# Two groups of zero matmuls, 55 of 128 columns, re-cut as 14 of 512 columns

## The chip, the cores and the metric

One core of a Trainium2 chip. The metric is device time in microseconds (us), the median of several executions; lower is better. "Span" is the stretch that the profile covers, about 2 us less than the time. An execution is "slow" when it lies over 1.5% above the fastest of its kernel; all comparisons below use fast executions. In the lines of the profile, PE is TensorE, PEld its weight loads, DVE VectorE, ACT ScalarE, POOL GpSimd and SP SyncE; L84 is line 84 of the kernel.

## The reference

A 3x3 convolution with padding 1, 16 images of 64 channels and 64x64 points, 128 output channels. The weights are 90% zeros, but the kernel treats them as dense.

```python
batch, c_in, h, w, c_out, k = 16, 64, 64, 64, 128, 3
for b, co, ci, kh, kw:   # five loops in the original
    if weight[co, ci, kh, kw] != 0:
        output[b, co] += weight[co, ci, kh, kw] * x_pad[b, ci, kh:kh+h, kw:kw+w]
```

x is 16.8 MB in f32, the output 33.6 MB in f32.

## The kernel before

Images are worked on in pairs, one on each half of TensorE's 128 rows. x is cast to bf16 while it is loaded, except the first 32 rows of the first pair, which are loaded as f32 and cast by VectorE and ScalarE, to be ready earlier. Before the first convolution the weights are loaded, cast, transposed on TensorE and combined. The parts concerned (cuts marked with ...):

```python
xs = [x_pool.tile([128, H, W], BF16, name=f"x{p}") for p in range(NP)]
...
nc.sync.dma_start(out=w_sb, in_=weight.rearrange("o i kh kw -> o (i kh kw)"))
x_head = o_pool.tile([128, H, W], FP32, name="o")
nc.sync.dma_start(out=x_head[:, 0:HEAD, :], in_=pair(0)[:, 0:HEAD, :])
nc.gpsimd.dma_start(out=xs[0][:, HEAD:H, :], in_=pair(0)[:, HEAD:H, :])
...
for p in range(1, EARLY):           # EARLY = 4
    load(p)
load(EARLY, 0, CUT)

idle_rhs = const_pool.tile([128, 128], BF16, name="idle_rhs")
nc.vector.memset(idle_rhs, 0.0)
idle_ps = psum_pool.tile([128, 128], FP32, name="ps")

def keep_busy(n):
    for _ in range(n):
        nc.tensor.matmul(idle_ps, idle_rhs, idle_rhs, start=True, stop=True)

keep_busy(27)                       # first group, while w is on its way
...                                 # casts and nine transposes of w
keep_busy(28)                       # second group, while x is on its way
cast_x(nc.scalar.copy, 9, 18)
...
for p in range(NP):                 # 8 pairs: convolution, then
    ...                             #   2 MB of output per image
            elif p > 1 and blk == 3 and p + EARLY - 1 < NP:
                load(p + EARLY - 1) # later loads are paced by the work
    if not last:
        for n in range(2):
            nc.sync.dma_start(out=out[2 * p + n], in_=o[n])
```

The zero matmuls write a tile in PSUM, the memory that takes the results of TensorE, and nobody reads it. They keep TensorE busy so that its clock is up when the convolution starts.

## Time and profile before

| | before |
|---|---|
| time, median (3 runs at first, then 6) | 126.27, 126.31 us |
| span of the profiled execution | 124.3 us |
| TensorE busy; VectorE busy | 88%; 66% |
| HBM traffic | 50.62 MB |
| convolution starts; last matmul ends | 7.38; 110.7 us |
| first output issued; last output issued | 21.86; 112 us |

The filler has these two rows among the groups (line, engine, operation, shape and count; busy us, mean ns of one; idle time before and what ended it):

```profile
L84 PE MATMUL ps<-idle_rhs 128*128 128x128 bf16 x55 | 4.8, 265 | 1.0 <-DVE idle_rhs L79 1.0
L84 PEld LDWEIGHTS <-idle_rhs 128*128 128x128 bf16 x55 | 4.4, 122 | 1.0 <-DVE idle_rhs L79 1.0
```

4.8 us of TensorE, every matmul with a weight load of its own. And one row of the DMA queues, to be compared later (queue, kind: transfers, MB, share of 16 engines): 8 blocks of 16 KB of instructions are fetched while the kernel runs.

```profile
q8 instruction: 8, 0.13, 0.4%
```

### The profile page before, as it was taken

What the parts mean: (1) busy time and instruction counts of PE and PEld (TensorE: products, weight loads), DVE (VectorE), ACT (ScalarE), POOL (GpSimd) and SP (SyncE); (2) the same over time, 40 slices, a digit from 0 to 9 for tenths busy, and PEclk for the clock granted to TensorE, in tenths of its full rate; (3) what the DMA queues carried; (4) which work ended last, traced back from release to release, by engine and by line L of the source; (5) the groups of instructions that cost most, each with busy time, mean ns of one, the idle gap of its engine ahead of it and who ended that gap; (6) DMA issues with size and microseconds to landing.
All of it is one profiled execution on the core that took longest, in us unless ns stands there. A gap on an engine that the chain in (4) does not pass through costs nothing.

```text
span 124.3 us, 2549 instructions
## 1 busy us (share of the span) xinstructions
PE 108.9 (88%) x1030; PEld 59.8 (48%) x1030; DVE 82.2 (66%) x135; ACT 39.0 (31%) x71; POOL 41.1 (33%) x46
## 2 busy tenths in 40 slices
PE   6989999999999999999999999999999999960000
PEld 6845555555555555555555555555555555520000
DVE  0354677877787778777877787778888788870000
ACT  4545323333333333333333333333333333310000
POOL 6428253533353335333533333343333310000000
PEclk9999999999999999999999999999999999998555
DMA  4999999999999999999999999999999999999991
GB/s 130 348 225 216 214 219 213 203 418 311 346 409 411 316 298 327 432 319 329 308 422 332 308 306 409 432 432 430 427 438 416 438 427 432 422 419 414 424 409 82
DMA packets 4196, 42.93 MB, mean 345 GB/s; under 512 B 472, under 2 KB 472, under 8 KB 984
## 3 DMA queue, kind: packets, MB, share of 16 engines
q1 hardware_dynamic: 2888, 34.90, 66.8%
q0 software_dynamic: 1296, 7.86, 30.8%
q8 instruction: 8, 0.13, 0.4%
q14 instruction: 4, 0.03, 0.1%
HBM read 17.07 MB, written 33.55 MB: 407 GB/s over the span
## 4 chain that ended last, share of the span: by engine, by line
PE 82%; DMA 5%; DVE 1%; issue 1%; DVEq 0%; SPq 0%
PE ps L148 82%; DMA o<-in_x_dram 5%; DVE o L181 1%; DVEq L240 0%; DVE x L99 0%; SPq L60 0%; DVEq L181 0%
## 5 line engine op out<-in xcount | busy, mean ns | idle before, releaser
L181 DVE TENSOR_TENSOR o<-ps,pc 128x512 f32<-128x512 f32 x124 | 77.7, 685 | 22.2 <-PE ps L148 19.8
L148 PE MATMUL ps<-x,wT 64*128 64x504 bf16 (+3 forms) x780 | 88.8, 373 | 0.6 <-DVE x L99 0.6
L148 PEld LDWEIGHTS <-wT 64*128 64x128 bf16 x966 | 54.8, 94 | 48.9 <-issue 0.6
L167 POOL TENSOR_TENSOR s<-x 128x512 bf16<-128x512 bf16 x31 | 35.5, 1149 | 57.6 <-PE ps L148 40.2
L174 ACT COPY pc<-ps 128x512 f32<-128x512 f32 x62 | 33.3, 590 | 64.0 <-issue 61.8
L148 PE MATMUL ps<-s,wT 64*128 64x512 bf16 (+1 forms) x186 | 25.7, 377 | 0.0
L84 PE MATMUL ps<-idle_rhs 128*128 128x128 bf16 x55 | 4.8, 265 | 1.0 <-DVE idle_rhs L79 1.0
L84 PEld LDWEIGHTS <-idle_rhs 128*128 128x128 bf16 x55 | 4.4, 122 | 1.0 <-DVE idle_rhs L79 1.0
L68 POOL DMA_DIRECT2D x<-in_x_dram x8 | 4.4, 559 | 0.0
L103 DVE CAST w_bf<-w_sb 128x192 bf16<-128x192 f32 (+1 forms) x4 | 1.1, 345 | 2.7 <-DMA w_sb<-in_weight_dram 2.7
L162 DVE COPY o<-ps 128x512 f32<-128x512 f32 x2 | 1.4, 692 | 2.0 <-PE ps L148 2.0
L161 ACT COPY o<-ps 128x512 f32<-128x512 f32 x2 | 1.2, 586 | 2.4 <-PE ps L148 2.4
L99 ACT CAST x<-o 128x576 bf16<-128x576 f32 (+1 forms) x2 | 1.5, 802 | 1.1 <-DMA o<-in_x_dram 1.1
L99 DVE CAST x<-o 128x576 bf16<-128x576 f32 x1 | 0.5, 459 | 2.1 <-DMA o<-in_x_dram 2.1
L103 ACT ACT_TABLE_LOAD x1 | 1.3, 1283 | 0.7 <-PEq L229 0.7
L103 ACT CAST w_bf<-w_sb 128x64 bf16<-128x64 f32 (+1 forms) x2 | 0.7, 416 | 1.6 <-DMA w_sb<-in_weight_dram 1.6
L109 PE MATMUL ps<-ident,w_bf 128*128 128x128 bf16 x9 | 1.0, 276 | 0.1
L113 DVE TENSOR_TENSOR wT<-ps,wT 128x384 bf16<-128x384 f32 x2 | 1.0, 546 | 0.0
L109 PEld LDWEIGHTS <-w_bf 128*128 128x128 bf16 x9 | 0.7, 120 | 0.5 <-DVE w_bf L103 0.5
L63 POOL DMA_DIRECT2D x<-in_x_dram x1 | 0.7, 693 | 0.8 <-POOLq L229 0.8
L79 DVE MEMSET idle_rhs<- 128x64 uint32 x1 | 0.1, 112 | 0.8 <-PEq L229 0.8
L122 ACT CAST wT<-ps 128x384 bf16<-128x384 f32 x1 | 0.5, 478 | 0.4 <-PE ps L109 0.4
(8 smaller groups left out, 1.9 us busy)
## 6 DMA issues: line engine op xcount, KB each, us to landing
out_dram<-o SPq DMA_DIRECT2D x14, 2048.0 KB, 17.9
x<-in_x_dram POOLq DMA_DIRECT2D x6, 1024.0 KB, 15.7
out_dram<-o SPq DMA_DIRECT2D x4, 1024.0 KB, 12.0
o<-in_x_dram SPq DMA_DIRECT2D x1, 1024.0 KB
x<-in_x_dram POOLq DMA_DIRECT2D x1, 640.0 KB, 14.3
x<-in_x_dram POOLq DMA_DIRECT2D x1, 512.0 KB, 7.6
x<-in_x_dram POOLq DMA_DIRECT2D x1, 384.0 KB, 25.2
w_sb<-in_weight_dram SPq DMA_DIRECT2D x1, 288.0 KB
```

The costliest lines, as they stand in the source:

```text
L68: nc.gpsimd.dma_start(out=xs[p][:, a:b, :], in_=pair(p)[:, a:b, :])
L84: nc.tensor.matmul(idle_ps, idle_rhs, idle_rhs, start=True, stop=True)
L99: copy(out=xs[0][:, a:b, :], in_=x_head[:, a:b, :])
L103: copy(out=w_bf4[:, g, a:b, :], in_=w_v[:, k : k + b - a, :])
L109: nc.tensor.matmul(wps[:, j, :], src, ident, start=True, stop=True)
L113: nc.vector.tensor_tensor(out=wT[:, g], in0=wps, in1=wT[:, G1], op=SUB)
L148: nc.tensor.matmul(ps[n][:, lo:hi, c_lo:c_hi], tap(g, kw, n), src[q, a:b:step, c_lo + kw - 1 : c_hi + kw - 1], start=(i == 0), stop=(i == ...
L161: nc.scalar.copy(out=o[0][:, r0 : r0 + rows, :], in_=ps[0])
L162: nc.vector.tensor_copy(out=o[1][:, r0 : r0 + rows, :], in_=ps[1])
L167: nc.gpsimd.tensor_tensor(out=s, in0=xs[p][:, r0 : r0 + 16 : 2, :], in1=xs[p][:, r0 + 1 : r0 + 16 : 2, :], op=ADD)
L174: nc.scalar.copy(out=c, in_=shared[n])
L181: nc.vector.tensor_tensor(out=o[n][:, first : r0 + 16 : 2, :], in0=ps[n], in1=pc[n], op=ADD)
```

## The change

The same busy time with fewer instructions: 7 + 7 matmuls of 512 columns (7168 columns) for 27 + 28 of 128 (7040). The weights of a zero matmul stay 128 columns.

```diff
-    idle_rhs = const_pool.tile([128, 128], BF16, name="idle_rhs")
+    idle_rhs = const_pool.tile([128, 512], BF16, name="idle_rhs")
     nc.vector.memset(idle_rhs, 0.0)
-    idle_ps = psum_pool.tile([128, 128], FP32, name="ps")
+    idle_ps = psum_pool.tile([128, 512], FP32, name="ps")
 
     def keep_busy(n):
         for _ in range(n):
-            nc.tensor.matmul(idle_ps, idle_rhs, idle_rhs, start=True, stop=True)
-
-    keep_busy(27)
+            nc.tensor.matmul(idle_ps, idle_rhs[:, 0:128], idle_rhs, start=True, stop=True)
+
+    keep_busy(7)
@@ after the transposes
-    keep_busy(28)
+    keep_busy(7)
```

## The prediction

> **What bounds the kernel now.** I read the page first for the transfers, because TensorE's 88% busy alone would suggest that TensorE sets the time. The rows of the 40 slices (3.1 us each), and what went to and from HBM:
>
> ```profile
> PE   6989999999999999999999999999999999960000
> DMA  4999999999999999999999999999999999999991
> GB/s 130 348 225 216 214 219 213 203 418 311 346 409 411 316 298 327 432 319 329 308 422 332 308 306 409 432 432 430 427 438 416 438 427 432 422 419 414 424 409 82
> HBM read 17.07 MB, written 33.55 MB: 407 GB/s over the span
> PE 82%; DMA 5%; DVE 1%; issue 1%; DVEq 0%; SPq 0%
> ```
>
> See three things. PE stops four slices before the end, while DMA is at 9 from the second slice to the last but one. The rate is about 215 GB/s where only loads run (slices 3 to 8) and about 425 where only outputs run. And the chain (last line, of its summary by engine) names PE for 82%, but it ends at the last compute instruction and says nothing of the 12 us after that. The 215 is not a slow DMA: x is loaded as f32 and lands as bf16, and the rate counts the bytes that land. HBM traffic is 50.62 MB (17.07 + 33.55) against 42.93 MB in the queues' total; the missing 7.69 MB is about the 7.86 MB of the converting queue, counted once instead of twice. So in HBM bytes the early rate is about 430 as well. 50.62 MB at 427 GB/s (the rate of a late slice) takes 118.5 us; the DMA begins to move at about 1.5 us and is done at about 122.5. That leaves some 2 us of 121 without full traffic. The transfers bound this kernel, not TensorE.
>
> Second, busy shares in four stretches (columns: stretch, length, the five compute engines in us with counts, granted clock, DMA share, GB/s):
>
> ```profile
> 1.50:24.50 23.00, 22.28 (x223) 13.78 (x223) 13.41 (x25) 9.19 (x17) 11.48 (x15) 1.00 1.02 232
> 24.50:61.00 36.50, 36.50 (x346) 19.40 (x344) 28.55 (x46) 12.67 (x24) 14.41 (x14) 1.00 1.02 354
> 61.00:105.00 44.00, 44.00 (x416) 23.37 (x414) 34.60 (x56) 14.22 (x28) 14.72 (x14) 1.00 1.01 400
> 105.00:120.00 15.00, 5.66 (x54) 2.78 (x50) 5.56 (x9) 2.12 (x4) 0.00 (x0) 0.80 1.00 422
> ```
>
> The next to last column is full in all four; in the last stretch PE works 5.66 of 15 us and the outputs drain.
>
> Third, the timeline of the start, where the change lies (start, duration, engine, line, operation; in brackets the idle time before it and what ended it):
>
> ```profile
> 0.82 0.11 DVE L79 MEMSET idle_rhs<- 128x64 uint32 x1 [0.82 <-PEq L229]
> 0.99 3.06 PE L84 MATMUL ps<-idle_rhs 128*128 128x128 bf16 x27 [0.99 <-DVE idle_rhs L79]
> 3.62 1.14 DVE L103 CAST w_bf<-w_sb 128x192 bf16<-128x192 f32 x4 [2.68 <-DMA w_sb<-in_weight_dram]
> 4.17 1.04 PE L109 MATMUL ps<-ident,w_bf 128*128 128x128 bf16 x9
> 5.05 1.73 PE L84 MATMUL ps<-idle_rhs 128*128 128x128 bf16 x28
> 6.87 0.46 DVE L99 CAST x<-o 128x576 bf16<-128x576 f32 x1 [2.11 <-DMA o<-in_x_dram]
> 7.38 3.99 PE L148 MATMUL ps<-x,wT 64*128 64x512 bf16 x36 [0.61 <-DVE x L99]
> ```
>
> The zero matmuls are not needed for any result; they fill the time in which weights and image arrive. The first 27 take 3.06 us, 113 ns each, and individually 314 ns from start to modelled end; the 28 later ones take 1.73 us, 62 ns each, individually 219 ns. The durations change among the nine transposes, so TensorE gets its full speed at about 4.9 us, though the granted clock reads 1.00 from the first slice: that column does not show this warm-up. PE then waits 0.61 us for the cast of x, which waited for its load to land at 6.85. This fixes 7.38 whatever the filler does, so long as the filler ends before it.
>
> **What the Trainium skill says.** "TensorE: Matmul & The Clock Gate", section "What's actually happening", says that the array runs at half clock until it has been busy for one window of about 3.4 us, and that the window runs freely. The trace agrees in size: busy from 0.99, fast at about 4.9, 3.9 us. Its section "Wait — 56ns, not 53.3ns?" gives the distance from start to start: N/1.2 ns cold and N/2.4 + 2.5 ns warm, so 107 and 56 ns for 128 columns, 427 and 216 ns for 512. The trace has 106 ns (3.06 less the last one's 0.31, over 26 distances) and 56 ns (1.73 less 0.22, over 27). For 512 columns I use the page's figures as estimates; nothing with 512 columns on the full array stands in this trace. "VectorE: DVE Perf Modes", section "Zero memsets can be issued as uint32 (trn2)", says one cycle per element: the trace shows the uint32 form, 64 elements in 112 ns. "DMA: Bandwidth & Descriptors", section "Where 436 GB/s comes from", puts the ceiling of the ports at 435 GB/s; slices at 427 to 438 are at it.
>
> **The change part by part.** It removes 55 zero matmuls (27 + 28), each with its weight load, and puts 14 (7 + 7) in their place. The columns streamed go from 7040 to 7168, nearly the same array time by design. PE gets 82 instructions fewer; ACT, POOL and SP keep the order they had; DVE gets only a larger memset.
>
> Memset: 256 elements in place of 64. 192 more elements at one cycle of the VectorE's 0.96 GHz (the specification in the skill's "Trainium Kernel Development and Optimization", NeuronCore Architecture) are 0.20 us, so 0.31 us. The first filler starts at about 1.19 in place of 0.99. DVE has nothing else until 3.62: no cost there.
>
> First filler: cold, 7 x 427 = 2.99 us from first start to the earliest next start, so the array is free at 4.18; before, 27 x 106 = 2.86, free at 3.85. The transposes, held until 4.17 by the cast of the weights, may start about 0.02 us later. On the path of PE, nothing worth a sum.
>
> Second filler: 7 x 216 = 1.51 us against 28 x 56 = 1.57. It starts at about 5.07, the array is free at 6.58 and the last one ends near 6.75 (before 6.78). Still ahead of 7.34, when the cast of x releases the convolution. PE's wait there goes from 0.61 to about 0.6 us.
>
> Sum on the path: 0 at the first real matmul, and hence 0 in every output's issue time. Total: 126.27 + 0.0.
>
> **The rivals.** *The clock warms one window later.* The filler starts 0.2 us later, and the window runs freely; if the start falls just outside a window, full speed comes at about 8.3 in place of 4.9 (one 3.41 us window more). Then the second filler is cold: 7 x 427 = 2.99 us from 5.07, to 8.06, and the convolution starts 0.7 us late. That would move the chain of PE by 0.7 us and a little more for a few slow matmuls, up to 1 us. For it: 3.9 us in the trace is 0.5 more than one window, so the window began at about 1.5 and 1.19 still lies before it, but other executions have other phases. Against any effect on time: the first output is issued at 21.86, and the DMA is still working on the loads issued at the start until about 24.5, when the rate goes from 160 to 393 GB/s. So 2.6 us of lateness is hidden there. At the other end, about 7.0 MB move after 105.0, of which 4.19 MB are the last pair's; the other 2.8 MB are a backlog of 6.7 us at that time. Worth: 0 to +0.3 us.
>
> *Fewer instructions help.* 82 fewer on PE, and their fetching, could free the start of a queue. But the loads of w and x are issued by SP and POOL at 0.74 to 4.6 us without waiting for PE, and instruction queues take 0.5% of the DMA. Worth: 0 to -0.2 us.
>
> *Fewer, longer matmuls count as less activity, or the clock falls between the last filler and the convolution.* The idle gap there stays 0.6 us, which before did no harm: the 36 matmuls after it take 3.99 us, 111 ns each, the pace of the whole kernel. If it did fall, some 3.4 us at half speed cost about 1.7 us of PE, again below the 2.6 us of slack. Worth: 0 to +0.5 us.
>
> **Range and chances.** All three rivals end at a full DMA queue, so the spread is that of executions: before has 126.22 to 126.40. Another build on another turn of the chip may lie some tenths away. I predict 126.25 us, 8 in 10 between 125.9 and 126.7. Over 2% either way is 2.5 us, for which I see no mechanism: faster by over 2% 0.005, within 0.99, slower 0.005.
>
> **What would show it right or wrong.** In the changed profile: the memset near 0.31 us; the first filler about 1.2 to 4.35 by its modelled end (seven of about 600 ns cold); transposes at 4.17 to 4.25; the second filler done before 6.9; the first real matmul at 7.38 within 0.1, released by the cast of x; DMA digits unchanged, end of traffic near 122.5. Wrong would be a first real matmul after 7.5 or the first 36 spread over clearly more than 4 us (late clock), and, if the time then moved by as much, my claim that the DMA queue hides it. A change of the time with an unchanged start would mean that I have mistaken what bounds the transfers.

## The result, and the profile after

126.35 us median of 6 runs (126.10 to 126.55) against 126.31 (126.22 to 126.42). The ratio is 1.000, 95% interval 0.9987 to 1.0013. Ratios here are the mean time of one kernel's fast runs over that of the other's of the same rounds, so not quite the ratio of the medians quoted.

The start after (timeline: start, duration, engine, line, operation):

```profile
0.86 0.27 DVE L79 MEMSET idle_rhs<- 128x256 uint32 x1 [0.86 <-PEq L229]
1.19 3.17 PE L84 MATMUL ps<-idle_rhs 128*128 128x512 bf16 x7 [1.19 <-DVE idle_rhs L79]
4.26 1.16 PE L109 MATMUL ps<-ident,w_bf 128*128 128x128 bf16 x9
5.26 1.67 PE L84 MATMUL ps<-idle_rhs 128*128 128x512 bf16 x7
7.38 3.99 PE L148 MATMUL ps<-x,wT 64*128 64x512 bf16 x36 [0.44 <-DVE x L99]
```

The filler starts 0.20 us later, the second group ends at 6.93, and the convolution starts at 7.38 as before, released by the same cast of x. Its first 36 matmuls take 3.99 us, as before: the clock is up. The stretches that the prediction shows, and the transfers (the page's row of DMA, then its row of the instruction queue):

```profile
1.50:24.50 23.00, 22.56 (x185) 11.41 (x185) 13.43 (x25) 9.20 (x17) 11.54 (x15) 1.00 1.02 232
105.00:120.00 15.00, 5.66 (x54) 2.78 (x50) 5.56 (x9) 2.11 (x4) 0.00 (x0) 0.82 0.99 421
DMA  4999999999999999999999999999999999999991
q8 instruction: 7, 0.11, 0.3%
```

The weight loads in the first stretch fall from 13.78 to 11.41 us; DMA share and rate stay. One thing differs that I had not counted: the instruction queue fetched 7 blocks of 16 KB instead of 8. It returns in the experiments.

### The profile page after: what moved, and what is told of

Same layout as the page of the kernel before. It is cut to its first block, busy times and chain, and to the rows that moved or that the text cites. A ratio compares the mean times of both kernels' runs of the same rounds, so it can differ in the third digit from the quotient of the medians.

```text
span 124.5 us, 2467 instructions
## 1 busy us (share of the span) xinstructions
PE 109.0 (88%) x989; PEld 57.1 (46%) x989; DVE 82.4 (66%) x135; ACT 39.0 (31%) x71; POOL 41.2 (33%) x46
## 4 chain that ended last, share of the span: by engine, by line
PE 82%; DMA 5%; DVE 1%; issue 1%; DVEq 0%; SPq 0%
PE ps L148 82%; DMA o<-in_x_dram 5%; DVE o L181 1%; DVEq L240 0%; DVE x L99 0%; SPq L60 0%; DVEq L181 0%
## 5 line engine op out<-in xcount | busy, mean ns | idle before, releaser
L181 DVE TENSOR_TENSOR o<-ps,pc 128x512 f32<-128x512 f32 x124 | 77.8, 685 | 22.1 <-PE ps L148 19.8
L84 PE MATMUL ps<-idle_rhs 128*128 128x512 bf16 x14 | 4.8, 505 | 1.2 <-DVE idle_rhs L79 1.2
L84 PEld LDWEIGHTS <-idle_rhs 128*128 128x128 bf16 x14 | 1.6, 121 | 3.2 <-issue 1.4
```

Source lines behind the costliest of these rows:

```text
L84: nc.tensor.matmul(idle_ps, idle_rhs[:, 0:128], idle_rhs, start=True, stop=True)
L181: nc.vector.tensor_tensor(out=o[n][:, first : r0 + 16 : 2, :], in0=ps[n], in1=pc[n], op=ADD)
```

## The experiments

The theory: the transfers run without a break from the start to the end, so the end moves only where the DMA stands idle; and the convolution's start is set by x, not by the filler. Main rival: TensorE sets the end. All kernels below are edits of the changed kernel unless stated. The kernel before ran beside each on the same chip; its median was 126.26, 126.36 and 126.34 us in the three batches.

### No filler at all

```diff
-    keep_busy(7)
+    keep_busy(0)
@@ second group
-    keep_busy(7)
+    keep_busy(0)
```

> Both zero-matmul groups removed (0 in place of 7 and 7); memset and tiles stay. Theory (the transfers bound the kernel, the start of the convolution has about 2.6 us of slack): TensorE is idle before 4.2 and from about 5.3 to 7.4, so the convolution starts at 7.38 but at half speed until one busy window of some 3.4 us has passed, up to two with the free phase; PE is 1.7 to 3.4 us late from then on, first output issued at 23.6 to 25.3 in place of 21.86; time +0.0 to +0.8 us. Rival (PE sets the end): time +1.7 to +3.4 us. Rival (the filler does nothing for the clock): first 36 matmuls still 4 us, no lateness, time +0.0.

Five fast runs of 126.42 to 128.22 us, one slow; ratio 1.0061 (1.0011 to 1.0111), some 0.8 us. In the profiled run (127.79 us):

```profile
4.27 1.22 PE L109 MATMUL ps<-ident,w_bf 128*128 128x128 bf16 x9 [4.27 <-DVE w_bf L103]
7.35 6.80 PE L148 MATMUL ps<-x,wT 64*128 64x512 bf16 x36 [1.85 <-DVE x L99]
```

The first 36 matmuls take 6.80 us in place of 3.99, so the filler is worth 2.8 us of TensorE in this execution; the first output is issued at 24.65, 2.8 us late. The span is 126.0, only 1.5 us more than the 124.5 of the changed kernel: part is hidden. The rival that the filler does nothing falls. The mean loss is inside my 0.0 to 0.8, but single runs are beyond it; the slack must be smaller than 2.6 us.

### Delays of the convolution

More zero matmuls in the second group delay the convolution. Its own matmuls then run at full speed (the first 36 in 3.98 us in all four). One thing besides changes: all four fetch 8 blocks of instructions, as the kernel before does, where the changed one fetches 7.

```diff
-    keep_busy(7)
+    keep_busy(17)    # delay_2;  29 in delay_4, 57 in delay_10, 14 in delay_1
```

> Second group 17 in place of 7: 10 x 216 ns more, array free at about 8.93, so the convolution starts 1.55 us later, at full speed. Theory: inside the slack of 2.6 us at the first output, time +0.0 (under 0.3 us). Rival (PE sets the end): +1.55 us, 1.2%.

> Second group 29 in place of 7: convolution starts at about 11.5, 4.1 us later, at full speed. Theory: 2.6 us of that are hidden, so +1.5 us (0.9 to 2.1). Rival (PE sets the end): +4.1. Rival (only the backlog of 6.7 us at the end is the slack): +0.0.

> Second group 57 in place of 7: convolution starts at about 17.6, 10.2 us later. Theory: the loads issued at the start are through at about 24.5, the first output is issued at about 32, so the DMA stands idle for 7.5 us and the end moves by as much: +7.5 us (7 to 8.3). Rival (PE sets the end): +10.2 us. Rival (only the backlog at the end counts as slack, 6.7 us at 105): +3.5 us.

> Second group 14 in place of 7: array free at about 8.3, convolution 0.9 us later. The runs with larger delays gave spans of first output issue + 101.3 to 101.6 us, against 124.3 to 124.5 without delay, so the slack at the first output is about 1.2 us, not 2.6. Theory with that slack: time +0.0 to +0.3. Rival (PE sets the end, the smaller gains being noise): +0.9 us.

| kernel | convolution starts | first output issued | span | span less first issue | median us | ratio to before |
|---|---|---|---|---|---|---|
| before | 7.38 | 21.86 | 124.3 | 102.4 | 126.31 | 1 |
| changed | 7.38 | 21.86 | 124.5 | 102.6 | 126.35 | 1.000 |
| delay_1 | 8.93 | 23.42 | 125.4 | 102.0 | 126.41 | 1.0019 |
| delay_2 | 8.79 | 23.28 | 124.9 | 101.6 | 126.83 | 1.0053 |
| no filler | 7.35 | 24.65 | 126.0 | 101.4 | 127.2 (fast) | 1.0061 |
| delay_4 | 11.90 | 26.39 | 127.7 | 101.3 | 129.56 | 1.0253 |
| delay_10 | 17.71 | 32.20 | 133.6 | 101.4 | 135.22 | 1.0719 |

The times in columns two to five are of the profiled execution, the last two of all runs. (That of delay_1 was one of two with an execution over 127 us: its second group started with slow matmuls, so the delay was 1.55 us there, not 0.9; the other four were 126.21 to 126.50. Delay_4 began its second group with slow matmuls too, and its delay was 4.5 us where 4.1 was expected; that of delay_10 was 10.3.) From a delay of 2.8 us on, the end follows the first output one to one, 101.4 us behind it. Without delay the end is at 124.4. The two meet at a first output at 124.4 - 101.4 = 23.0 us: the slack is about 1.2 us, not 2.6. Delay_4 was outside my 0.9 to 2.1 (it cost 3.2 us), delay_10 outside my 7 to 8.3 (it cost 9.1); "TensorE sets the end" would have been 4.1 and 10.2, "only the backlog at the end counts" 0 and 3.5. Delay_2 was to cost under 0.3 us and cost 0.6. Each of these numbers misses. On delay_4 and delay_10 mine miss by 1.7 and 1.6 us, and those of "TensorE sets the end" by only 0.9 and 1.1, so these two numbers alone do not decide for me. What speaks against that rival is that about the same 1.2 us is missing from both (4.5 and 10.3 us of measured delay, 3.2 and 9.1 of cost) and that it had 1.55 for delay_2; the next experiment tests it directly. A slack of 1.2 us fits delay_4 and delay_10 within 0.2 and delay_2 within 0.4. The traced execution of delay_1 ends 0.6 us later than this slack gives; why is open.

Where the missing 1.4 us of slack lie shows the idle DMA of delay_10 (stretches: as above, the last two columns are DMA share and GB/s):

```profile
22.00:23.00 1.00, 1.00 (x12) 0.45 (x10) 0.45 (x1) 0.94 (x3) 0.49 (x1) 1.00 0.81 162
24.00:25.00 1.00, 1.00 (x14) 0.41 (x12) 1.00 (x3) 0.00 (x0) 0.00 (x0) 1.00 0.64 123
25.00:26.00 1.00, 1.00 (x12) 0.48 (x10) 1.00 (x3) 0.38 (x1) 0.24 (x1) 1.00 0.03 6
32.20:33.00 0.80, 0.80 (x11) 0.39 (x8) 0.51 (x1) 0.80 (x2) 0.80 (x1) 1.00 0.00 0
33.00:34.00 1.00, 1.00 (x14) 0.49 (x10) 0.69 (x2) 0.14 (x1) 0.83 (x2) 1.00 1.25 524
```

Between the issue of the first output at 32.20 and the first traffic at 33.0 lie 0.8 us, which I had left out; and the engines run dry unevenly before 24.5 (share 0.81 between 22 and 23, 0.64 between 24 and 25). The first is measured; that the second makes the remaining 0.6 us is the rest of the sum, not measured by itself.

### Less to load

Pairs 4 to 7 use the images of pairs 0 to 3 again. The result is wrong (relative error 1.0); all compute instructions and outputs stay, 8.4 MB of HBM reads go.

```diff
-    xs = [x_pool.tile([128, H, W], BF16, name=f"x{p}") for p in range(NP)]
+    xs = [x_pool.tile([128, H, W], BF16, name=f"x{p}") for p in range(4)]
+    xs = xs + xs
@@
-    load(EARLY, 0, CUT)
@@ and the two later calls of load in the loop over pairs
```

> Wrong result on purpose: pairs 4 to 7 use the images of pairs 0 to 3 again, so 8.4 MB less is read from HBM; every compute instruction and every output stays. Theory: PE keeps its times (convolution 7.38 to about 110), but the DMA has no backlog left; the last two outputs are issued at 111.4 to 112 and 2.1 MB at 427 GB/s end them at about 117 in place of 122.4; time 121.0 us, -5.3. Rival (PE sets the end also in the kernel as it is): time unchanged, within 0.5 us.

123.17 us, ratio 0.9757: faster by 3.1 us with the work of TensorE untouched (first output at 22.07, even 0.2 later). Where the 0.2 us come from, the trace shows:

```profile
5.16 2.49 PE L84 MATMUL ps<-idle_rhs 128*128 128x512 bf16 x7
6.70 0.46 DVE L99 CAST x<-o 128x576 bf16<-128x576 f32 x1 [1.96 <-DMA o<-in_x_dram]
7.58 3.98 PE L148 MATMUL ps<-x,wT 64*128 64x512 bf16 x36
```

In this execution full speed came only at about 6.8 us. The second group took 2.49 us in place of 1.67 and held the convolution until 7.58, although x was cast at 7.16. So TensorE does not set the end of the real kernel; this rival falls. But 5.3 was too much. I had forgotten pair 6: its outputs are issued at 98.85, and from there 8.4 MB are still to be written, which at 423 GB/s is 19.8 us (99.65 with the 0.8 us of start-up, to 119.5). Measured: 421 GB/s from 99.5 to 119.0, 344 until 119.5, and next to nothing after (17 and 16 GB/s until 120.5). Even here the last 20 us are of transfers; what TensorE sets is when they begin.

> The cut of loads (pairs 4 to 7 use the images of 0 to 3, wrong on purpose) without any zero matmul. Theory: with no backlog in the DMA, PE's lateness comes through; time 1.7 to 3.4 us over the kernel with cut loads and filler, i.e. about 122.7 to 124.4 if that is 121.0. Rival (filler worthless for the clock): same as with filler.

125.30 us (124.65 to 126.19), ratio to before 0.9920 against 0.9757 with filler: 2.1 us more, on another chip of the same kind. The first output came 2.26 us later (24.33), the span is 2.2 longer (123.9 against 121.7). Without a backlog, TensorE's lateness comes through in full, as expected.

### Both fillers with less to load

Here the cut of loads is made in the kernel before, and compared with the cut in the changed kernel.

> The cut of loads (wrong on purpose) with the filler of before, 27 and 28 matmuls of 128 columns. Theory: both fillers end before the cast of x frees the convolution at 7.38 and both have the clock up, so even where PE's time comes through, the two fillers cost the same: within 0.3 us of the cut kernel with 14 of 512. Rival (only the DMA hides a difference of the two fillers): a difference of over 0.5 us shows here.

124.32 us, 1.15 over the 14-matmul version, where I had expected under 0.3. The two had run on different chips, so both ran again on one:

> The kernel with cut loads and 14 zero matmuls of 512 once more, beside the next one on one chip, because the two filler variants with cut loads ran on different chips and differed by 1.1 us while their first outputs were issued within 0.3 us. Theory (that difference is of chip or execution, not of filler): the two within 0.3 us here. Rival (fewer instructions, and so one instruction fetch less among the transfers, help where the loads are cut): this one faster by about 0.6 us or more again.

> Cut loads with the filler of before, 27 and 28 of 128 columns, beside the last one. Theory: within 0.3 us of it. Rival: slower by 0.6 to 1.1 us, with a longer tail of one or two DMA engines at the end of the trace.

123.17 (123.11 to 123.83) against 124.26 (124.09 to 124.46): ratios to before 0.9762 and 0.9836. My theory, that chip or execution made the difference, falls; the shorter instruction stream is faster by 1.1 us here. In the two traces, first output 22.45 and 21.66, the last 23 us differ. (The whole spans hide it, 122.1 and 122.2: the traced execution with 14 was its slowest, 123.83 us, with x late and the convolution at 7.97, against 7.18 in the one with 55.) The kernel with 14 (transfers from 98.5 to 122, rates in slices of 0.59 us, and its instruction queues):

```profile
GB/s 0 0 446 446 418 335 335 446 363 363 418 446 446 446 446 446 446 446 446 279 363 446 446 432 432 418 418 377 404 404 446 446 432 432 418 390 153 14 0 0
q14 instruction: 1, 0.01, 0.1%
```

and with 55:

```profile
GB/s 0 446 446 446 446 446 446 446 446 446 418 390 390 335 390 307 418 446 404 432 432 404 432 376 390 404 446 446 432 432 418 404 432 404 404 42 42 28 0 0
q8 instruction: 1, 0.02, 0.2%
q14 instruction: 1, 0.01, 0.1%
```

With 55, queue 8 fetches one 16 KB block of instructions in this stretch, and the transfers end with three slices at 28 to 42 GB/s, one or two of the 16 engines still at work while the others are done. With 14 there is no such fetch, and the tail is one slice at 14. The fetch falls between 107 and 108 us; a query of that one microsecond gives

```profile
q8 instruction: 1, 0.02, 5.8%
```

5.8% of 16 engines for 1 us are 0.93 us of one engine. The Trainium skill, "Runtime: NRT & Kernel Launch", section "Instruction fetch mechanics", says that an engine's instruction memory is refilled by its own DMA queue in blocks of 16 KiB, 256 instructions each, at a cost that is mostly hidden. That fits one block fewer in a stream that is 82 instructions shorter (the traces show 7 and 8); that it is hidden does not hold here. From the first issue of pair 6's outputs to the end of the span it is 22.9 us with 14 (98.85 to 121.7 and 99.23 to 122.1) and 23.8 us with 55 (98.56 to 122.3 and 98.43 to 122.2): 0.9 us. The kernel with cut loads and no filler, which has no such fetch either, takes 22.8 (101.10 to 123.9). In all 14 traces the count goes with the length of the program: 7 fetches up to 2467 instructions, 8 from 2481. Size, place and tail agree with one engine delayed by one fetch. No run moved a fetch alone, so this cause is matched, not isolated.

Why then do the two kernels with all loads take the same time, though the one before has 8 fetches and the changed one 7? There the DMA has been full since the start, and its end is ragged anyway: in the kernel before, the rate falls from 393 GB/s at 120 to 121 us over 254 to 33 at 122.5 to 123. A fetch on an engine that would have finished early would cost nothing; whether that is the reason I could not tell, since what I read does not say which engine ends last. That it costs nothing there the delays show: delay_4 and delay_10 have an eighth fetch in the last stage (between 114 and 118 us), the kernels without filler and without the second group have none after 104 us, and all four end 101.3 to 101.4 us after their first output.

### One group of the two, and 14 short ones

```diff
@@ second group
-    keep_busy(7)
+    keep_busy(0)
```

> First group of 7 stays, second removed, loads as they are. Theory: full speed comes at about 5.2 during the transposes; the idle time from 5.4 to 7.38 is 2 us, shorter than a window, so the convolution still starts fast: first 36 matmuls in about 4 us, time +0.0. Rival (the second group is what keeps or brings the clock up): first 36 in 6 to 8 us, PE 1.7 us or more late, first output at 23.5 or later; the time then still under +0.8 us by the slack.

126.80 us (126.69 to 126.97), ratio 1.0039, some 0.5 us. My theory for this run falls: the clock went as the rival has it, and the time stayed under the rival's 0.8 us. The trace shows it well (stretches; the column of 1.00 and 0.50 is the granted clock):

```profile
1.00:4.40 3.40, 3.21 (x9) 0.98 (x10) 0.78 (x3) 1.67 (x3) 3.08 (x7) 1.00 0.79 265
4.40:7.85 3.45, 1.28 (x15) 0.78 (x17) 1.48 (x6) 2.03 (x5) 0.21 (x1) 1.00 1.03 270
7.85:11.25 3.40, 3.40 (x20) 1.60 (x18) 1.25 (x3) 0.94 (x2) 2.79 (x3) 0.50 1.07 223
11.25:14.65 3.40, 3.40 (x35) 1.77 (x32) 1.00 (x2) 1.69 (x4) 1.38 (x2) 1.00 1.05 219
```

The stretches are cut at the changes of the clock; the first one, from slow to fast, does not show in the column. TensorE is fast from about 4.3 us here. It then works 1.28 of 3.45 us, with no idle time longer than the 2.15 us before the convolution, and is put back to half clock at 7.85, with the convolution already running. It stays there for 3.40 us. So in this execution the second group is missed not for bringing the clock up but for keeping it. That is not always its part: the first matmul starts at 1.19 us in every traced kernel that has the 512-column groups, but full speed came at about 4.3 us here and in delay_2, at 5.2 in the changed kernel, and at about 6.0, 6.3 and 6.8 in delay_4, delay_1 and the one with less to load, during the second group. The first 36 matmuls take 5.67 us and the first output is 1.68 us late.

The kernel before with `keep_busy(7)` twice has 14 matmuls of 128 columns:

```diff
-    keep_busy(27)
+    keep_busy(7)
@@ second group
-    keep_busy(28)
+    keep_busy(7)
```

> 14 zero matmuls, 7 and 7, but of 128 columns: the count of the new kernel with a quarter of its columns, and the memset of 64. Theory (what counts is the array's busy time): first group busy for some 0.8 us from 0.99, second for 0.4 to 0.8, so the full speed comes only during the convolution; PE 1.5 to 3 us late, first output at 23.4 to 25, time +0.3 to +2.0 us. Rival (the number of matmuls or merely some activity is enough): first 36 in 4 us, no lateness, +0.0.

Fast runs 126.65 to 128.00 us, ratio 1.0077 (1.0047 to 1.0108), 1.0 us: as costly as no filler. The count does not do it. That it is the busy time, or the shorter gaps that go with it, is read from the time alone: the profiled execution was a slow one, with x landing late, so nothing of it is used.

## Why the prediction was right

**The bound.** Right. With 8.4 MB less to read the time falls by 3.1 us at unchanged compute, and a late TensorE costs nothing while it stays within the slack, 1.2 us. The margin is narrow: beyond it the end follows TensorE one to one.

**The sum of the start.** Right where it counts, the unmoved convolution. Memset 0.27 us where I had 0.31; the 192 more elements took 0.16 us, not 0.20. First start 1.19 as predicted, but partly by luck: the larger memset also started 0.04 us later (0.86 against 0.82). Start to start of the 512-column matmuls is 423 ns cold ((3.17 - 0.634) / 6) and 215 warm ((1.67 - 0.379) / 6), against 427 and 216 estimated; one alone takes 634 and 379 ns. Transposes at 4.26 were 0.09 later than before, since the cast of w came 0.09 later. They ran slow for longer, and the second group came at 5.26 instead of 5.07 and ended at 6.93, past the 6.9 that I had set as a sign. The wait before the convolution is 0.44 in place of 0.6 us, and its start is unmoved.

**The rival "one window later".** It did not occur in the profiled run; clock-up was at about 5.2. But the first trace with less to load, whose start is the same, shows its mechanism: clock-up at about 6.8, the filler ending after x was ready, the convolution 0.2 us late where I had put 0.7. So "0 on the path" holds for the profiled execution and not for every one; what covers the others is the slack. Its worth of up to 0.3 us rested on the slack.

**The slack of 2.6 us.** Wrong in size: 1.2 us. I had taken the first output's issue for the beginning of its traffic (0.8 us later) and the loads' last moment for the moment at which engines begin to stand idle. The prediction survived because the change moved the convolution by nothing, so the slack was never drawn on.

**The rival "fewer instructions help".** I looked at the start of the queues and gave it 0 to -0.2 us. With all loads it is 0 (within 0.2 us). With the loads cut it is -1.1 us, and the likely cause is a fetch at the end, a place that I had not looked at.

**The rival of less activity.** The 14 long matmuls count as the 55 short ones did. My ground in the prediction, that this gap would stay about as short as the one before, held: 0.44 us did no harm. What fell is the ground that I gave later, for the run without the second group, that a gap shorter than a window does none: 2.15 us of gap with 1.28 us of work in 3.45 us lost the clock. The size of such a loss was right: 1.7 us estimated, the first output 1.68 late.

No version with the right result beat both kernels. Fewer bytes would shorten the real one, by 3.1 us in the test above; an earlier first byte might, which was not tested. The changed kernel is as fast as the one before, with 82 fewer instructions on TensorE.

## What to carry to other kernels

A chain that names TensorE for 82% ends at the last compute instruction; look at what the transfers do after it, and count HBM bytes over the rate before calling an engine the bound. Where filler keeps the clock up, size it by time and keep the gaps short: here 14 long matmuls did the same as 55 short ones, with fewer instructions. When the clock comes up late the filler itself runs longer, so leave room between its end and the first real matmul. When a slack is to hide something, count it from the first traffic, not from the issue, and test it with a series of known delays: the kink gives its size.

## What the Trainium skill lacked or had wrong

- "TensorE: Matmul & The Clock Gate", "What's actually happening": gives at least one idle window for the way back to half clock. Here 1.28 us of work in 3.45 us, with the longest idle time 2.15 us, was enough; the half clock then lasted 3.40 us, one window, which agrees. The page has no figure for how little work in a window keeps the clock up.
- The same page warns that the clock events of traces cannot be fully trusted, but does not say that the granted clock in a profile reads 1.00 through the first slow stretch: cold matmuls of 634 ns stand under 1.00 at 1.2 to 4.4 us, while the later fall reads 0.50.
- "VectorE: DVE Perf Modes", "Zero memsets can be issued as uint32 (trn2)": one cycle per element would be 0.20 us for 192 more elements; measured 0.16 us (112 to 272 ns), the same in every trace. Its end came 0.20 later, since the larger one also started 0.04 later.
- "Runtime: NRT & Kernel Launch", "Instruction fetch mechanics": calls the cost of a fetch mostly hidden. For TensorE it was: in the kernel before, it is busy for 44.00 of the 44.00 us from 61 to 105, in which fetches fall. But the 16 KB transfer holds one DMA engine for about 0.93 us, and at the end of a transfer-bound kernel one fetch more went with 0.9 us of span where loads were cut, and with none where they were not; the page does not count it against the other transfers.
